# Mixed decoder layer on one core: heads of the scores in turn, a GpSimd drain, and other places for ten tiles' weight sums

## The chip, the cores and the metric

The kernel runs on one core of a Trainium2 chip. A core has five engines, each with its own instruction stream: TensorE (PE in the profile, with PEld for its weight loads), VectorE (DVE), ScalarE (ACT), GpSimd (POOL) and SyncE (SP), which issues most of the DMAs. The engines meet only at semaphores. The metric is the device time of one execution in microseconds (us); less is better.

## The reference

The program is one decoder layer on 512 tokens of 1024 features, all in float32. It has three parts, each with a normalisation before and after it and added to the input:

- a SwiGLU network ("first FFN"): `(silu(x @ w_gate) * (x @ w_up)) @ w_out`, with 2816 inner features, added by half;
- a token mixer: one projection `h @ w_in` to 3592 columns feeds four HGRN2 heads (a gated recurrence with a decay per feature) and four mLSTM heads (a gated recurrence with a stabilised exponential gate, query and key of 64 features, values of 128); both are causal. Their normalised, gated outputs go through `w_out`;
- a second FFN like the first.

For an mLSTM head the reference computes, chunk by chunk, with `D` made of the cumulated gates:

```
P = einsum("bhtd,bhsd->bhts", qc, kc) * exp(D - m_t)
num = inter * (qc @ C) + P @ vc
```

The product of `qc` and `kc` is what is called the scores here.

## The kernel before, in words

All products are made of float32 operands split into two parts of a rounded format ("high" and "low"), and three products high x high, high x low, low x high are added in PSUM. So every weight tile of 512 KB is loaded by SP into a raw buffer (line 242), cast by ScalarE (line 279, the high part) and subtracted by VectorE (line 281, the low part) into one of four prepared weight buffers, before TensorE uses it. `weights` plans the loads: each raw buffer belongs to a ring of three or five, and a load is issued when the buffer's last reader is done.

Both FFNs save products by Strassen-like sums, with seven products instead of eight. In the input products (`ffn_in`, `prod`, matmuls of line 602) the sums of weight tiles are made in SBUF by `tensor_tensor` additions of raw buffers (lines 291 to 295): VectorE makes most of them, GpSimd those of the first tiles. In the output products (`ffn_out`, `quartered`, lines 920 and 928) sums of quarters of weight tiles are needed, thirteen tiles for each FFN: eight for the first half of the output columns, five for the second. These are not made in SBUF. `sums_ahead` copies four quarters from the weights in DRAM into a DRAM buffer (`f1sums`, `f2sums`; three DMAs on SP, lines 868 to 870) and adds other quarters to it by three accumulating DMAs, each of which GpSimd issues (line 873) after the one before it has landed. A normal weight load brings the finished sums in later.

`sums_ahead` is a generator with four steps: copies, then one accumulate per step. `sums_due` names the tiles that are due, and each call of `make_sums` starts one more tile and takes one step of each tile in work. Before the change, the first FFN makes its thirteen tiles in its own products; the second FFN's first eight are made in the mixer (calls in the jobs for the convolution, `hi` and `mv`), and its last five in its own input products (every tenth product, `EVERY`) and at the start of its output products.

The order on each engine is the order in which the program's functions call the instructions; `behind` puts an instruction behind another one in that order (line 496). `self.loaded` is the last load issued so far.

The mixer runs a queue of "jobs", which are generators for the projection's products (`job_f`, `job_t`, matmuls of lines 185 to 187 and 532), and calls `fill(n)` to place `n` pieces of them between steps of the recurrences, so that TensorE has work. `mlstm_scores` goes through the four heads; the generator `mlstm_head` makes the exponential of a head's gates first (a matmul by `neg_m` at line 1489, VectorE, ScalarE, then GpSimd's `affine_select` at line 1515 as causal mask), then four 128x128 score products of 64 partitions at line 1523, and then the product of both on VectorE (line 1525). Heads 0 and 2 lie on partitions 0 to 63, heads 1 and 3 on 64 to 127. PSUM has eight banks, given out in turn by `ps`.

In `masks` GpSimd prepares constants for the mixer; the last instruction there is the copy at line 1236.

At the end of each half of the output products `rms` (lines 436 to 441) takes squares on ScalarE, whose sums GpSimd scales into small column tiles, for the normalisation.

Of the kernel before, what the change touches and what calls it, by code (L numbers as in the profile page):

```python
# [11 lines left out]
ALU = mybir.AluOpType  # L12
# [72 lines left out]
PLACES, LATER = {2: 1, 4: 2, 6: 0, 8: 3}, {7: (2, 3)}  # L85

AGAIN, ROWS = (10,), (18, 19, 20, 21)
EVERY = 5, 10

# [25 lines left out]
class Layer:  # L117
# [122 lines left out]

    def load(self, ld):
        self.loaded = self.nc.sync.dma_start(self.raw[ld.key], ld.src)

    def lie(self, kind):

# [10 lines left out]
    def split(self):  # L256

        nc = self.nc
        it = self.items.popleft()
        raw = self.raw[it.key]  # L260
        _, a, b = raw.shape
        if it.dst:
            w = it.dst()
        else:
            if self.wt is None:
                self.wt = self.wp.tile([P, 2 * D * WBUF + FRONT + PAD], F32R, name="w")
            if not self.slot and it.key[0] != "mix":
                self.free = deque(FREE2 if it.key[0] == "f2" else FREE)
            n, o = self.lie("out" if it.key[1] == "out" else "mix" if it.key[0] == "mix" and b == 512 else "any")
            self.free.remove(n)  # L270
            w = self.wt[:, o : o + 2 * D].rearrange("p (b k t) -> p b k t", b=2, k=a)
            self.slot[id(w)] = n, o, w
        hi, lo = self.both(w)
        if it.sums:
            raw, hi, lo = (self.flat(v)[:, QUARTER:] for v in (raw, hi, lo))
        self.ready.append((w, it.dst is not None))
        rows = it.rows
        if rows is None:
            nc.scalar.copy(hi, raw)  # L279
            yield  # L280
            self.low = nc.vector.tensor_tensor(lo, raw, hi.bitcast(F32), op=ALU.subtract)  # L281
        else:
            for j in range(a):
                nc.scalar.activation(hi[:, j], raw[:, j], AF.Copy, scale=rows[:, j : j + 1])
            yield
            for j in range(a):
                nc.vector.scalar_tensor_tensor(
                    lo[:, j], raw[:, j], rows[:, j : j + 1], hi[:, j].bitcast(F32), op0=ALU.mult, op1=ALU.subtract
                )
        with self.behind(*self.hold):  # L290
            for out, other in it.adds:
                o, c = self.raw[out], self.raw[other]

                late = out[1] >= (HEAD if out[0] == "f1" else 1)
                (nc.vector if late else nc.gpsimd).tensor_tensor(o, o, c, op=ALU.add)  # L295
        self.load_due(self.done)
        self.done += 1
        yield
# [482 lines left out]

    def ffn_in(self):

        self.sums_due("f2" if self.second else "f1", (1,) if self.second else (0, 1))
        for n, (p, t) in enumerate(ORDER2[len(HEADS2) :] if self.second else ORDER[len(HEADS) :]):
            if n > 14 and n % EVERY[self.second] == 0:
                self.make_sums()
            with self.behind(*(self.c22 if p == "p3" and self.second else ())):
                self.feed()
            self.c22 = []  # L790
            self.lag()
            self.prod(p, t)
            self.after(p, t)
            if t == PAIRS - 1 and p in ("p3", "p7"):
                self.hs.append(self.h_tile(len(self.hs)))
        self.feed()
        self.lag()
# [61 lines left out]
        parts = [t.rearrange("p k (c u t) -> p k u c t", u=2, t=P) for t in parts]  # L859
        return [[t[:, j // 2, j % 2] for j in range(4)] for t in parts]  # L860

    def sums_ahead(self, f, h, k2):

        nc, to = self.nc, self.sums_of[f, h, k2]
        w = (self.ffn1_w_out, self.ffn2_w_out)[f == "f2"][0]
        q = w[k2 * 2 * P : (k2 + 1) * 2 * P, h * 512 : (h + 1) * 512].rearrange("(k p) (c f) -> p k c f", p=P, f=QUARTER)
        with self.behind(self.loaded):
            nc.sync.dma_start(to[:, 0], q[:, 0, 1])
            nc.sync.dma_start(to[:, 1], q[:, 1, 0])
            nc.sync.dma_start(to[:, 2:], q[:, 1])  # L870
        yield
        for a, b, v in ((0, 2, q[:, 0, :1].broadcast_to([P, 2, QUARTER])), (2, 3, to[:, :1]), (3, 4, to[:, 2:3])):
            nc.gpsimd.dma_start(to[:, a:b], v, accum_op=ALU.add)  # L873
            yield

    def sums_due(self, f, halves):
        self.ahead, self.making = deque(k for k in self.sums_of if k[0] == f and k[1] in halves), []

    def make_sums(self):

        if self.ahead:
            self.making.append(self.sums_ahead(*self.ahead.popleft()))
        self.making = [g for g in self.making if next(g, self) is not self]

    def ffn_out(self, gpost_row, scale, after, trans, head):
# [81 lines left out]

        with self.behind(*([self.loaded] if self.second else [])):
            g = self.gain("gpost", gpost_row)
        n = 0  # L970
        for half in range(2):
            C = [[self.ps() for _ in range(2)] for _ in range(2)]
# [32 lines left out]
        for k2 in OUT[1][-LAST:]:  # L1005
            ws.append(self.pull())
            more(n + 1)
            n += 1
        hs = [made.popleft()[0] for _ in range(LAST)]

        add(C, T, 1)

# [33 lines left out]
    def job_f(self, name, then):  # L1046

        w, ps = self.pull(), self.ps()
        if name[0] == "c":
            self.make_sums()  # L1050
        for k in range(ND):
            self.in_k(ps, w, k, [(0, HALF), (HALF, T)])
            if k < ND - 1:
                yield
        self.drop(w)
        then(ps)
        self.got.add(name)
        yield
# [148 lines left out]
    def masks(self, mc, mb):  # L1207

        nc = self.nc

        self.mask = mb.tile([P, len(LEVELS), 64], I32, name="mask")
        nc.gpsimd.memset(self.mask, 1)
        for n, c in enumerate(LEVELS):
            m = self.mask[:, n, :].rearrange("p (b c) -> p b c", c=c)
            pat = [[-2 * c, 64 // c], [0, c]]
            nc.gpsimd.affine_select(m, m, pattern=pat, compare_op=ALU.is_ge, fill=0.0, base=0, channel_multiplier=1)
            pat = [[2 * c, 64 // c], [0, c]]
            nc.gpsimd.affine_select(m, m, pattern=pat, compare_op=ALU.is_ge, fill=0.0, base=c - 1, channel_multiplier=-1)
        self.eye = mb.tile([P, P], I32, name="eye")
        nc.gpsimd.memset(self.eye, 1)  # L1220
        nc.gpsimd.affine_select(
            self.eye, self.eye, pattern=[[1, P]], compare_op=ALU.is_equal, fill=0.0, base=0, channel_multiplier=-1
        )

        sel = mb.tile([4, 6, 2, 64], F32, tag="tmp", bufs=1, name="sel")
        nc.gpsimd.memset(sel, 1.0)
        self.sel = mc.tile([36, 6, P], F32R, name="selr")
        nc.gpsimd.memset(self.sel.bitcast(I32), 0)
        for n in range(6):
            pat = [[0, 2], [0, 64]] if n < 4 else [[-1, 2], [0, 64]]  # L1230
            base = -n if n < 4 else -2 * (n - 4)
            nc.gpsimd.affine_select(
                sel[:, n], sel[:, n], pattern=pat, compare_op=ALU.is_equal, fill=0.0, base=base, channel_multiplier=1
            )
        for r in (0, 32):
            nc.gpsimd.tensor_copy(self.sel[r : r + 4], sel.rearrange("p n a b -> p n (a b)"))
    def forget_gates(self, mb):

        nc = self.nc
# [187 lines left out]
    def job_rows(self):  # L1427

        ps = self.ps()[:100]
        for k in range(ND):  # L1430
            for n in range(2):
                for m in range(2):
                    v = slice(HALF * m, HALF * (m + 1))
                    self.nc.tensor.matmul(
                        ps[:, v], self.gw[:, k, :], self.xop(k, n, HALF * m, HALF * (m + 1)),
                        start=k + n + m == 0, stop=k == ND - 1 and n == 1, skip_group_check=True,
                    )
            if k % 2 == 1 and k < ND - 1:
                yield
# [64 lines left out]
    def mlstm_head(self, h):  # L1504
# [16 lines left out]
        for c in range(NT):  # L1521
            s = slice(c * P, (c + 1) * P)
            nc.tensor.matmul(sc[:, s], self.qk[o : o + 64, 2 + h // 2, s], self.qk[o : o + 64, h // 2, s], start=True, stop=True)  # L1523
        yield
        nc.vector.scalar_tensor_tensor(self.pT[:, h, :], sc, 0.125, e, op0=ALU.mult, op1=ALU.mult)
        yield

    def mlstm_scores(self, mc):
# [2 lines left out]
        self.nend = mc.tile([P, NH, NT], F32, name="nend")  # L1531
        self.pT = mc.tile([P, NH, T], F32, name="pT")
        H = [self.mlstm_head(h) for h in range(NH)]
        next(H[0])
        for h in range(NH):
            if h + 1 < NH:
                next(H[h + 1])
            self.fill(3)
            next(H[h])
            next(H[h])  # L1540
        w = mc.tile([P, NT, NH], F32, name="w")
        nc.vector.tensor_tensor(w, self.aT, self.nend.rearrange("p h c -> p c h"), op=ALU.add)
        nc.scalar.activation(w, w, AF.Exp)
# [127 lines left out]
    def mixer(self):  # L1671
        nc, tc = self.nc, self.tc
        self.got, self.jobs = set(), deque()
        self.sums_due("f2", (0,))
        with tc.tile_pool(name="ma", bufs=1) as ma:
            self.vh = ma.tile([P, NT, NH, P], F32, name="vh")
            self.vm = ma.tile([P, NT, NH, 129], F32, name="vm")
# [187 lines left out]
```

## Time and profile before

| what | value |
|---|---|
| three timed runs | 936.67, 940.88, 942.86 us (median 940.88) |
| the profiled execution | 936.0 us |
| its span, first to last instruction | 934.3 us |
| granted TensorE clock | 0.998 |
| DMA traffic | 142.28 MB, 152 GB/s in the mean |
| DMA issued by GpSimd (q0) | 13.64 MB, 11.2% of 16 engines |

The stages in the profiled execution: the first FFN's input products from the start to 224 us (first matmul of line 920), its output products and the norm behind them to 340 (first matmul of line 542), the mixer to about 600, the second FFN's input products to about 813, its output products to 927 (last matmul of line 920), and the last normalisation and stores.

The page has a line of busy time for each engine, the span in 40 slices, DMA queues, a chain of work followed back from the last instruction, and the costliest groups of instructions. Matmuls are pipelined and their ends are modelled, so TensorE's busy share alone does not say whether it runs at its pace; the number of matmuls in a stretch does. "idle before" is the time in which an engine did nothing ahead of an instruction, with what ended it.

### The profile page before, as it was taken

The numbers are of one execution on the slowest core, as the hardware profiler recorded it, in microseconds if no ns is written. First come the engines' busy times: TensorE is split into PE (matmuls) and PEld (weight loads), VectorE is DVE, ScalarE is ACT, GpSimd is POOL, SyncE is SP. The second block draws the span as 40 slices with busy tenths as digits, with TensorE's granted clock in tenths as the row PEclk, the third lists the DMA queues.
The fourth block names the chain that finished last, engine by engine and source line by source line (L and its number), as shares of the span: only waits on it lengthen the run. The fifth ranks groups of instructions, "written<-read, shape, count | busy, mean of one in ns | idle before, by whom it ended". The sixth has DMA issues, their size and how long they took to land.

```text
span 934.3 us, 18295 instructions
## 1 busy us (share of the span) xinstructions
PE 922.8 (99%) x7435; PEld 887.7 (95%) x7435; DVE 759.2 (81%) x980; ACT 521.5 (56%) x751; POOL 179.5 (19%) x250
## 2 busy tenths in 40 slices
PE   9999999999999999999999999999999999999996
PEld 7999999999999999998888887899999999999996
DVE  6899988889887786698766555799899889988883
ACT  7646455557566457956523345594445545756641
POOL 3531112211111045222230310313010010100001
PEclk9999999999999999999999999999999999999999
DMA  9255778766996234477742125253376556467522
GB/s 315 70 152 143 187 206 194 193 147 160 241 276 215 81 98 123 121 176 160 170 87 63 45 90 175 88 166 93 97 192 171 150 159 198 132 193 224 175 74 91
DMA packets 116494, 142.28 MB, mean 152 GB/s; under 512 B 7189, under 2 KB 89657, under 8 KB 116410
## 3 DMA queue, kind: packets, MB, share of 16 engines
q1 hardware_dynamic: 101562, 126.95, 43.8%
q0 software_dynamic: 14560, 13.64, 11.2%
q8 instruction: 58, 0.95, 0.4%
q10 hardware_dynamic: 288, 0.52, 0.2%
q14 instruction: 26, 0.21, 0.1%
HBM read 138.99 MB, written 29.36 MB: 180 GB/s over the span
## 4 chain that ended last, share of the span: by engine, by line
PE 54%; DVE 5%; issue 2%; DMA 2%; POOL 1%; ACT 1%; DVEq 0%; POOLq 0%; ACTq 0%
PE ps L602 14%; PE ps L928 7%; PE ps L532 6%; PE ps L920 5%; PE ps L185 5%; PE ps L187 5%; PE ps L186 5%; DVE w L281 2%; PE ps L1342 2%; DMA raw<-in_ffn_w_in_dram 2%; DVE raw L295 1%; PE ps L347 1%; POOL raw L295 1%; PE ps L542 1%; PE ps L1523 0%
## 5 line engine op out<-in xcount | busy, mean ns | idle before, releaser
L279 ACT CAST w<-raw 128x1024 fp32r<-128x1024 f32 x244 | 249.6, 1029 | 195.8 <-PE ps L602 85.5
L281 DVE TENSOR_TENSOR w<-raw,w 128x1024 fp32r<-128x1024 f32 x244 | 297.5, 1222 | 32.8 <-ACT w L279 31.5
L602 PE MATMUL ps<-xq,w 128*128 128x256 f32 x2016 | 237.3, 277 | 0.0
L602 PEld LDWEIGHTS ps<-xq,w 128*128 128x128 f32 x2016 | 232.9, 188 | 0.1
L602 PE MATMUL ps<-sq,w 128*128 128x256 f32 x1512 | 178.2, 276 | 2.2 <-DVE ps L621 1.8
L602 PEld LDWEIGHTS ps<-sq,w 128*128 128x128 f32 x1512 | 174.3, 188 | 3.2 <-issue 2.0
L295 DVE TENSOR_TENSOR raw<-raw,raw 128x1024 f32<-128x1024 f32 x72 | 89.8, 1251 | 11.8 <-DMA raw<-in_ffn_w_in_dram 10.3
L920 PE MATMUL ps<-w,hs 128*128 128x256 f32 x768 | 91.2, 276 | 0.0
L920 PEld LDWEIGHTS ps<-w,hs 128*128 128x128 f32 x768 | 88.9, 188 | 0.0
L185 PE MATMUL ps<-w,xq 128*128 128x512 f32 x192 | 78.0, 407 | 0.1
L928 PE MATMUL ps<-w,hs 128*128 128x256 f32 x624 | 75.0, 276 | 0.0
L186 PE MATMUL ps<-w,xq 128*128 128x512 f32 x192 | 74.9, 391 | 0.0
L187 PE MATMUL ps<-w,xq 128*128 128x512 f32 x192 | 74.8, 391 | 0.0
L928 PEld LDWEIGHTS ps<-w,hs 128*128 128x128 f32 x624 | 72.7, 188 | 0.0
L532 PE MATMUL ps<-xq,w 128*128 128x256 f32 x480 | 55.7, 277 | 0.0
L532 PEld LDWEIGHTS ps<-xq,w 128*128 128x128 f32 x480 | 54.9, 188 | 0.5 <-issue 0.5
L814 ACT CAST hs<-hf 128x1024 fp32r<-128x1024 f32 x34 | 35.8, 1053 | 34.2 <-PE ps L928 22.3
L815 DVE TENSOR_TENSOR hs<-hf,hs 128x1024 fp32r<-128x1024 f32 x34 | 41.5, 1221 | 11.9 <-ACT hs L814 11.5
L873 POOL DMA_DIRECT2D f1sums<-f1sums x26 | 22.8, 879 | 111.7 <-DMA f1sums<-in_ffn_w_out_dram 53.1
L185 PEld LDWEIGHTS ps<-w,xq 128*128 128x128 f32 x192 | 36.1, 188 | 8.5 <-issue 0.9
L187 PEld LDWEIGHTS ps<-w,xq 128*128 128x128 f32 x192 | 36.0, 188 | 8.1 <-DVE xq L354 0.3
L873 POOL DMA_DIRECT2D f2sums<-in_ffn_w_out_dram x13 | 17.3, 1333 | 137.3 <-DMA f2sums<-in_ffn_w_out_dram 137.3
(262 smaller groups left out, 1201.6 us busy)
## 6 DMA issues: line engine op xcount, KB each, us to landing
raw<-in_ffn_w_in_dram SPq DMA_DIRECT2D x98, 512.0 KB, 4.9
raw<-in_ffn_w_out_dram SPq DMA_DIRECT2D x44, 512.0 KB, 4.5
raw<-in_w_mix_in_dram SPq DMA_DIRECT2D x28, 512.0 KB, 4.1
raw<-f1sums SPq DMA_DIRECT2D x13, 512.0 KB, 7.5
raw<-f2sums SPq DMA_DIRECT2D x13, 512.0 KB, 4.5
raw<-in_w_mix_out_dram SPq DMA_DIRECT2D x8, 512.0 KB, 4.3
f1sums<-in_ffn_w_out_dram SPq DMA_DIRECT2D x26, 128.0 KB, 4.4
f1sums<-in_ffn_w_out_dram SPq DMA_DIRECT2D x13, 256.0 KB, 5.5
```

The source lines that it names most:

```text
L185: mm(ps, sh, mh, start=start, stop=False, **kw)
L186: mm(ps, sh, ml, start=False, stop=False, **kw)
L187: mm(ps, sl, mh, start=False, stop=stop, **kw)
L279: nc.scalar.copy(hi, raw)
L281: self.low = nc.vector.tensor_tensor(lo, raw, hi.bitcast(F32), op=ALU.subtract)
L295: (nc.vector if late else nc.gpsimd).tensor_tensor(o, o, c, op=ALU.add)
L532: mm(ps[:, u0:u1], w[:, a, k, :], self.xop(k, b, u0, u1), start=k + n + m == 0, stop=k == ND - 1 and n == 2, skip_group_check=True,)
L602: self.nc.tensor.matmul(ps[:, c], wb[b][:, k, v], left[d][:, k, :], start=first and a + n + k == 0, stop=n == 2 and k == KH - 1, skip_grou ...
L815: self.nc.vector.tensor_tensor(lo, src, hi.bitcast(F32), op=ALU.subtract)
L873: nc.gpsimd.dma_start(to[:, a:b], v, accum_op=ALU.add)
L920: mm(out, a[kk][:, i * P : (i + 1) * P], w[:, b, kk, QUARTER * v : QUARTER * (v + 1)], start=begin and c == kk == n == 0, stop=kk == 1 and ...
L928: mm(ps[:, QUARTER * c : QUARTER * (c + 1)], A[a][:, c], B[b], start=begin and c == n == 0, stop=n == 2, skip_group_check=True,)
```

## The change

The scores' products of two heads alternate, chunk by chunk, and the gates of the next two heads come ahead of them. Of the second FFN's thirteen tiles of sums, the copies for five are issued at the end of the first FFN, behind its last output weight load; their accumulates, and five more whole tiles, run in the mixer; all accumulates for the second FFN stand behind the masks. The last three tiles run in the second FFN's output products, and its input products make none. A drain instruction stands on GpSimd in the second FFN's input products, behind its weight additions.

```diff
-EVERY = 5, 10
+EVERY, EARLY, AHEAD = 5, 5, 10
...
     def load(self, ld):
         self.loaded = self.nc.sync.dma_start(self.raw[ld.key], ld.src)
+        if ld.key[:2] == ("f1", "out"):
+            self.loaded1 = self.loaded
...
                 late = out[1] >= (HEAD if out[0] == "f1" else 1)
-                (nc.vector if late else nc.gpsimd).tensor_tensor(o, o, c, op=ALU.add)
+                added = (nc.vector if late else nc.gpsimd).tensor_tensor(o, o, c, op=ALU.add)
+                if not late:
+                    self.added = added
...
     def ffn_in(self):
-        self.sums_due("f2" if self.second else "f1", (1,) if self.second else (0, 1))
+        nc = self.nc
+        if not self.second:
+            self.begun = ()
+            self.sums_due("f1")
         for n, (p, t) in enumerate(ORDER2[len(HEADS2) :] if self.second else ORDER[len(HEADS) :]):
-            if n > 14 and n % EVERY[self.second] == 0:
+            if n > 14 and n % EVERY == 0 and not self.second:
                 self.make_sums()
+            if n == 14 and self.second:
+
+                with self.behind(self.added):
+                    nc.gpsimd.drain()
...
-    def sums_ahead(self, f, h, k2):
+    def sums_ahead(self, f, h, k2, early=False):
         nc, to = self.nc, self.sums_of[f, h, k2]
-        w = (self.ffn1_w_out, self.ffn2_w_out)[f == "f2"][0]
+        w, last = (self.ffn1_w_out, self.ffn2_w_out)[f == "f2"][0], self.loaded1 if early else self.loaded
...
-        with self.behind(self.loaded):
+        with self.behind(last):
             nc.sync.dma_start(to[:, 0], q[:, 0, 1])
             nc.sync.dma_start(to[:, 1], q[:, 1, 0])
             nc.sync.dma_start(to[:, 2:], q[:, 1])
         yield
         for a, b, v in ((0, 2, q[:, 0, :1].broadcast_to([P, 2, QUARTER])), (2, 3, to[:, :1]), (3, 4, to[:, 2:3])):
-            nc.gpsimd.dma_start(to[:, a:b], v, accum_op=ALU.add)
+            with self.behind(*([self.selected] if f == "f2" else [])):
+                nc.gpsimd.dma_start(to[:, a:b], v, accum_op=ALU.add)
             yield
-    def sums_due(self, f, halves):
-        self.ahead, self.making = deque(k for k in self.sums_of if k[0] == f and k[1] in halves), []
+    def sums_due(self, f, n=None, done=0):
+        self.ahead, self.making = deque([k for k in self.sums_of if k[0] == f][done:n]), []
+
+    def copies_early(self):
+
+        self.begun = deque(self.sums_ahead(*k, early=True) for k in [k for k in self.sums_of if k[0] == "f2"][:EARLY])
+        for g in self.begun:
+            next(g)
     def make_sums(self):
-        if self.ahead:
+        if self.begun:
+            self.making += [self.begun.popleft() for _ in range(min(2, len(self.begun)))]
+        elif self.ahead:
             self.making.append(self.sums_ahead(*self.ahead.popleft()))
         self.making = [g for g in self.making if next(g, self) is not self]
...
     def ffn_out(self, gpost_row, scale, after, trans, head):
...
+        if self.second:
+            self.sums_due("f2", done=AHEAD)
...
         hs = [made.popleft()[0] for _ in range(LAST)]
+        if not self.second:
+            self.copies_early()
...
     def job_f(self, name, then):
-        if name[0] == "c":
+        if name in ("conv0", "conv1", "conv2", "conv3"):
             self.make_sums()
...
-            nc.gpsimd.tensor_copy(self.sel[r : r + 4], sel.rearrange("p n a b -> p n (a b)"))
+            self.selected = nc.gpsimd.tensor_copy(self.sel[r : r + 4], sel.rearrange("p n a b -> p n (a b)"))
...
     def job_rows(self):
         ps = self.ps()[:100]
+        self.make_sums()
...
     def mlstm_head(self, h):
...
             nc.tensor.matmul(sc[:, s], self.qk[o : o + 64, 2 + h // 2, s], self.qk[o : o + 64, h // 2, s], start=True, stop=True)
-        yield
+            yield
...
     def mlstm_scores(self, mc):
         H = [self.mlstm_head(h) for h in range(NH)]
         next(H[0])
-        for h in range(NH):
-            if h + 1 < NH:
+        next(H[1])
+        for h in range(0, NH, 2):
+            self.fill(3)
+            for g in H[h + 2 : h + 4]:
+                next(g)
+            self.fill(3)
+            for _ in range(NT + 1):
+                next(H[h])
                 next(H[h + 1])
-            self.fill(3)
-            next(H[h])
-            next(H[h])
...
     def mixer(self):
         self.got, self.jobs = set(), deque()
-        self.sums_due("f2", (0,))
+        self.sums_due("f2", AHEAD, EARLY)
```

## The prediction

> **What bounds the kernel now.** I read the page first, then busy time by stretches, then the waits.
>
> ```profile
> span 934.3 us, 18295 instructions
> ...
> PE 922.8 (99%) x7435; PEld 887.7 (95%) x7435; DVE 759.2 (81%) x980; ACT 521.5 (56%) x751; POOL 179.5 (19%) x250
> ```
>
> TensorE is the bound by its busy share, but ends of matmuls are modelled, so I check it by counts. Columns of the next view: stretch, its length, then busy time and (number of instructions) of PE, PEld, DVE, ACT, POOL, then clock, DMA share, GB/s.
>
> ```profile
> 60.00:300.00 240.00, 240.00 (x2117) 240.00 (x2116) 213.72 (x242) 135.70 (x178) 38.93 (x47) 1.00 0.76 199
> 304.00:340.00 36.00, 35.92 (x316) 35.72 (x316) 27.71 (x39) 18.49 (x41) 7.75 (x19) 1.00 0.17 50
> 380.00:405.00 25.00, 25.00 (x219) 24.52 (x218) 20.00 (x25) 19.70 (x24) 3.02 (x3) 1.00 0.52 130
> 660.00:750.00 90.00, 89.82 (x787) 89.31 (x786) 83.49 (x90) 45.27 (x55) 5.75 (x6) 1.00 0.52 141
> 750.00:780.00 30.00, 28.01 (x243) 27.45 (x242) 25.93 (x28) 13.05 (x16) 2.84 (x3) 1.00 0.64 179
> 780.00:815.00 35.00, 35.00 (x311) 35.00 (x310) 33.87 (x43) 24.05 (x34) 4.01 (x4) 1.00 0.56 153
> ```
>
> In the first FFN, 240 us hold 2117 matmuls: 0.1134 us each, without a hole. That is the pace to measure by. At it, 660 to 750 should hold 794 and holds 787 (0.8 us lost); 750 to 780 should hold 265 and holds 243 (2.4 us lost, 2.0 of them plainly idle). The granted clock is 1.00 throughout. So there is little to win: no matmul is removed, and only idle time of TensorE can go. The waits of PE name the one long one:
>
> ```profile
> PE ps L602 <- DVE ps L621: 1.8, 1, 1.8
> ```
>
> VectorE was late once, in the second FFN, where it is busy 25.93 + 33.87 of 65 us (92%) from 750 to 815. Why it was late is in the order of time there (start, length, engine, line; in brackets the idle time before it and what ended it):
>
> ```profile
> 749.31 0.51 SPq L868 DMA_DIRECT2D f2sums<-in_ffn_w_out_dram  x1
> ...
> 750.50 0.60 SPq L870 DMA_DIRECT2D f2sums<-in_ffn_w_out_dram  x1
> ...
> 752.49 20.68 SPq L242 DMA_DIRECT2D raw<-in_ffn_w_in_dram  x7
> ...
> 754.47 1.17 POOL L873 DMA_DIRECT2D f2sums<-in_ffn_w_out_dram  x1 [22.61 <-DMA f2sums<-in_ffn_w_out_dram]
> ...
> 759.96 1.23 DVE L295 TENSOR_TENSOR raw<-raw,raw 128x1024 f32<-128x1024 f32 x1 [3.50 <-DMA raw<-in_ffn_w_in_dram]
> ```
>
> Three copies for one tile's sums stand on SP from 749.31 to 751.10, the weight loads behind them go on at 752.49, an accumulating DMA joins at 754.47, and VectorE's add then waits 3.50 us for a weight load. The 1.8 us wait of TensorE follows some ten microseconds later.
>
> **The change, part by part.** The base is the profiled execution: 936.0 us, of which the span is 934.3. The median of the three runs, 940.88, is 4.9 above it.
>
> *Sums out of the second FFN's input products.* Four sets of three copies and twelve accumulating DMAs leave the stretch from 683 to 800; SP's weight loads then follow each other there unbroken. The hole above goes: **-2.0 us**. It is bounded by 0 (the load would have been late anyway: only one of the four sets led to a hole) and by -3.2 (2.4 + 0.8, all that both stretches lost).
>
> *Scores of two heads in turn.* The products of 64 partitions (heads 0 and 2 in the lower half, 1 and 3 in the upper) now alternate between the halves.
>
> ```profile
> L1523 PE MATMUL ps<-qk 64*128 64x128 f32 x32 | 4.6, 285 | 0.0
> ...
> L1388 PE MATMUL ps<-q,kk 128*128 128x128 f32 x32 | 3.9, 275 | 0.0
> ```
>
> ```profile
> L1523 PE MATMUL ps<-qk x32: 272/272/373, 486.5 to 497.7; 64*128 64x128 f32 x32
> ```
>
> ```profile
> 490.10 0.74 PEld L1523 LDWEIGHTS ps<-qk 64*128 64x128 f32 x6 [0.35 <-issue]
> ```
>
> Head by head, 32 of them take 4.6 us, no less than 32 of full height (3.9). No row shows halves in turn. If a pair ran beside each other, half would go: -2.3. If each change of half cost what the longest of a group has over the shortest (373 - 272 ns), the 28 changes more would add 2.8. The nearest rows, those of L1523 itself, say neither gain nor loss; since each pair shares no partition and no bank, I take some overlap, **-1.0**. The visits to such small products between the projection's matmuls fall from six to five; one begins with 0.35 us of idle weight loading: **-0.2** (0 to -0.35). Queued behind the later scores are VectorE's four multiplies into pT; they share the order with one weight split, which four prepared weight buffers cover.
>
> The Trainium skill, TensorEngine Tiling (Array Packing), Key Properties, says that tiles of the array on different rows can load weights and multiply in parallel, and that a change of the tiling mode drains the array. By it this term would be about -2.3 (an estimate), 1.3 below what I take; no run here shows it yet.
>
> *Five tiles copied early.* Fifteen DMAs go to SP behind the first FFN's last weight load:
>
> ```profile
> 303.88 2.26 SPq L242 DMA_DIRECT2D raw<-in_ffn_w_out_dram  x1
> 340.96 0.37 SPq L242 DMA_DIRECT2D raw<-in_w_mix_in_dram  x1
> ```
>
> ```profile
> raw<-in_w_mix_in_dram SPq DMA_DIRECT2D x28, 512.0 KB, 4.1
> ...
> f2sums<-in_ffn_w_out_dram SPq DMA_DIRECT2D x13, 256.0 KB, 5.7
> f2sums<-in_ffn_w_out_dram POOLq DMA_DIRECT2D x13, 256.0 KB, 6.1
> f2sums<-f2sums POOLq DMA_DIRECT2D x26, 128.0 KB, 4.1
> ```
>
> SP is idle from 306.1 to 340.96, and the DMA share from 304 to 340 is 0.17. At 0.6 us an issue they need 9 us; even five sets landing one after another (5 x 5.7) end 6 us before the next load. **0**; were they later than that, the first mixer loads would be late by the excess.
>
> *Thirty accumulates in the mixers, not 24.* They stay behind the masks on POOL, where they stood before:
>
> ```profile
> 377.65 3.29 POOL L1236 CAST selr<-sel 4x768 fp32r<-4x768 f32 x2
> 394.95 1.24 POOL L873 DMA_DIRECT2D f2sums<-in_ffn_w_out_dram  x1 [14.02 <-DMA f2sums<-in_ffn_w_out_dram]
> ...
> 484.44 0.94 POOL L873 DMA_DIRECT2D f2sums<-f2sums  x1 [2.59 <-ACT vm L1696]
> 485.42 1.40 POOL L1548 MEMSET C<- 128x1548 f32 x1
> 486.77 0.83 POOL L1515 TENSOR_SCALAR_AFFINE_SELECT e<-e 128x512 f32<-128x512 f32 x1
> ```
>
> POOL sat 14.02 us until copies came; now five tiles lie ready at 381, and their accumulates need not wait for each other. Behind them POOL has C's memset and the selects for the scores; they have been kept until 485, and six more accumulates of 1 us with a 14 us earlier start end no later. The new thing is the burst at 381: four or five accumulates at once beside weight loads. A weight gives 48 matmuls, 5.4 us; with three raw buffers a load has 16 us, of which it needs 4.1. Even doubled it stays hidden: **0**, at most +2 where one load would take over 16.
>
> *Three tiles in the output products.* The trace has this case: the first FFN issues its last three sets in the same turns.
>
> ```profile
> 226.54 0.50 SPq L868 DMA_DIRECT2D f1sums<-in_ffn_w_out_dram  x1
> ...
> 251.65 0.65 SPq L868 DMA_DIRECT2D f1sums<-in_ffn_w_out_dram  x1
> ```
>
> ```profile
> 232.95 1.17 POOL L873 DMA_DIRECT2D f1sums<-in_ffn_w_out_dram  x1 [7.18 <-DMA f1sums<-in_ffn_w_out_dram]
> ...
> 280.60 0.81 POOL L873 DMA_DIRECT2D f1sums<-f1sums  x1 [5.91 <-DMA f1sums<-f1sums]
> 281.17 0.48 POOL L437 TENSOR_SCALAR col<-col 128x1 f32<-128x1 f32 x1
> ```
>
> ```profile
> 240.00:281.00 41.00, 41.00 (x364) 41.00 (x363) 35.81 (x42) 25.25 (x31) 6.95 (x8) 1.00 0.95 271
> ```
>
> Nine accumulates take 47.7 us, and TensorE has 364 matmuls in 41 us, its full pace, at a DMA share of 0.95. So **0**. The next rival says what it costs when this cover is gone.
>
> *The drain.* One POOL instruction, with no semaphore, behind the four adds; POOL then idles anyway:
>
> ```profile
> 689.16 1.25 POOL L873 DMA_DIRECT2D f2sums<-in_ffn_w_out_dram  x1 [45.06 <-DMA f2sums<-in_ffn_w_out_dram]
> ```
>
> It fits into 45 us: **0**.
>
> Sum: 936.0 - 2.0 - 1.0 - 0.2 = **932.8** on the profile's scale. What puts the other runs up to 6.9 above it (942.86 - 936.0) the trace cannot show. If it is late weight loads like the one above, the median comes down to 932.8; if it is something else, it stays 4.9 higher, 937.7. I take the middle, **935**.
>
> **The rivals.**
>
> *Everything pays.* Pairs overlap fully (-2.3, -0.35), both FFN stretches fill up (-3.2), and the runs' spread goes with them: 936.0 - 5.9 = 930.1. For it: the cause at 749 is plain. Against it: small waits of TensorE on VectorE stay.
>
> *Nothing but the scores.* VectorE at 92% is late by itself, and the hole moves to the next late load: 936.0 - 1.2 = 934.8 as profiled, 939.7 as a median. For it: VectorE also waited for loads around 653, with no copies near.
>
> *POOL's chain ends too late (slower).* Place: the end of the output products' first half, where POOL's small sums stand behind the ninth accumulate, and ScalarE's squares behind those (twelve column buffers, two to a square: six squares run free).
>
> ```profile
> 870.20 0.19 POOL L437 TENSOR_SCALAR col<-col 128x1 f32<-128x1 f32 x1 [46.08 <-ACT junk L436]
> ```
>
> ```profile
> 815.40 0.42 SPq L158 DMA_DIRECT2D gpost<-in_norm_post_dram  x1
> ```
>
> The last row is that of the first FFN's sums, all their DMAs together, from issue to landing:
>
> ```profile
> DMA to landing us min/median/max: 3.1/5.7/9.6
> ```
>
> The first set follows the load at 815.40 and lands by 822; at 5.3 us a step (47.7 / 9) the chain ends at 870, as POOL is first asked. Up to 7 us a step (885) prepared weights, three or four at 5 us, cover it. At the longest landing, 9.6 plus 1 for the issue, it ends at 917: 917 - 885 = 32 us lost, 936.0 - 3.2 + 32 = 965. From 7.4 us a step on (889, 4 lost against 3.2 won) the change is slower than before. Against it: the first FFN, at a fuller DMA, did it in 5.3.
>
> The Trainium skill, DMA: Bandwidth & Descriptors, Queues, rings and completion order, has each DMA engine alternate between its queues by packets, so that accumulates and loads slow each other. The trace agrees in part: all DMAs of the first FFN's sums land at a median of 5.7 us, at 9.6 at the longest.
>
> **How the numbers follow.** Forecast, 931.5 to 938: 0.50. Everything pays, 929 to 931.5: 0.28. Nothing but the scores, 938 to 943: 0.12. POOL's chain, 943 to 965: 0.10. The range 929 to 943 leaves out the last and the edge of the second. One per cent, about what a measurement of this kernel can tell from no change, is 9.4 us: 931.5 and 950.3. So faster 0.28, same 0.62, slower 0.10.
>
> **What would show it.** Right: 265 matmuls in each 30 us from 680 to 800 and no wait of PE on L621 over 1 us; scores' 32 products under 4 us busy; POOL's first accumulate at 381; SP copies at 304 to 316 with no hole of TensorE at 340. Wrong: POOL's first column sum after 875; a wait of TensorE between 381 and 420; weight loads of the second FFN still landing late without any copies near.

## The result, and the profile after

The changed kernel takes 932.64 us (median of six runs, 932.12 to 934.34), the kernel before 938.96 beside it. The ratio is 0.9931, 95% interval 0.9908 to 0.9954: 6.3 us faster, less than one per cent. In two later comparisons on other chips it was 0.9947 (0.9929 to 0.9965) and 0.9944 (0.9923 to 0.9965), a gain of 4.5 and 5.1 us, so about 5 us is the better figure. The profiled execution took 932.28, 3.7 less than that of before.

The head of the page, changed kernel:

```profile
span 930.6 us, 18289 instructions
...
PE 921.0 (99%) x7435; PEld 886.6 (95%) x7435; DVE 759.3 (82%) x980; ACT 521.7 (56%) x751; POOL 178.4 (19%) x250
```

The same matmuls are there, so the gain has to be idle time. Busy time by stretches, changed kernel (columns as in the prediction):

```profile
304.00:340.00 36.00, 36.00 (x318) 35.85 (x316) 27.67 (x39) 18.57 (x40) 7.74 (x19) 1.00 0.46 128
380.00:405.00 25.00, 25.00 (x217) 24.52 (x217) 20.00 (x25) 19.78 (x23) 15.10 (x16) 1.00 1.02 182
660.00:750.00 90.00, 89.91 (x791) 89.69 (x790) 84.42 (x90) 46.59 (x56) 0.00 (x0) 1.00 0.40 123
750.00:780.00 30.00, 28.99 (x251) 28.43 (x250) 26.60 (x28) 13.31 (x16) 0.00 (x0) 1.00 0.46 142
780.00:815.00 35.00, 35.00 (x311) 35.00 (x310) 33.91 (x44) 23.57 (x33) 0.00 (x0) 1.00 0.39 113
815.00:870.00 55.00, 55.00 (x488) 55.00 (x487) 47.39 (x61) 33.59 (x47) 9.28 (x12) 1.00 0.90 254
```

GpSimd has left the second FFN's input products from 660 on, but 750 to 780 holds 251 matmuls, not the 265 of full pace; before, 243. By idle time about half of the hole is still there (1.01 us of 1.99), by matmuls 14 of 22. The wait of TensorE on VectorE is 0.8 us instead of 1.8, because VectorE still waits 2.82 us for a weight load (3.50 before), though no copy is near (waits of PE, then the order of time):

```profile
PE ps L606 <- DVE ps L625: 0.8, 1, 0.8
```

```profile
757.51 1.23 DVE L297 TENSOR_TENSOR raw<-raw,raw 128x1024 f32<-128x1024 f32 x1 [2.82 <-DMA raw<-in_ffn_w_in_dram]
```

To find all of the 3.7 us I set pieces of the chain that ended last beside each other, pieces that both kernels have. First the kernel before, then the changed one (start, length, piece):

```profile
353.17 32.64 PE ps L532 x288
...
600.31 2.82 PE ps L602 x24
...
826.90 38.08 PE ps L928 x336
...
899.66 27.21 PE ps L920 x240
```

```profile
353.57 32.64 PE ps L536 x288
...
599.31 2.82 PE ps L606 x24
...
824.46 38.08 PE ps L948 x336
...
897.22 27.21 PE ps L940 x240
```

The differences, after minus before:

| from | to | difference in the stretch |
|---|---|---|
| start | the mixer's first products, 353 | +0.40 |
| there | the second FFN, 600 | -1.40 |
| there | its output products, 827 | -1.44 |
| there | its last 240 products, 900 | 0.00 |
| there | the end of the span | -1.26 |

The second row holds the scores, the third the input products that the sums have left. The +0.40 of the first is there long before the first edit has an effect: the 501st matmul starts at 65.07 in the kernel before and at 65.47 in the changed one, and in all traces here at 64.82 to 66.36. The last row is a surprise: nothing that the prediction priced lies behind 900.

### The profile page after: what moved, and what is told of

Its sections match the earlier page's. It is cut to its first block, busy times and chain, and to the rows that moved or that the text cites. A ratio compares the mean times of both kernels' runs of the same rounds, so it can differ in the third digit from the quotient of the medians.

```text
span 930.6 us, 18289 instructions
## 1 busy us (share of the span) xinstructions
PE 921.0 (99%) x7435; PEld 886.6 (95%) x7435; DVE 759.3 (82%) x980; ACT 521.7 (56%) x751; POOL 178.4 (19%) x250
## 4 chain that ended last, share of the span: by engine, by line
PE 58%; DVE 2%; DMA 2%; issue 1%; ACT 1%; POOL 0%; DVEq 0%; POOLq 0%; ACTq 0%; SPq 0%
PE ps L606 19%; PE ps L948 7%; PE ps L536 6%; PE ps L940 5%; PE ps L185 5%; PE ps L186 4%; PE ps L187 4%; PE ps L1366 2%; DMA raw<-in_ffn_w_in_dram 2%; DVE w L283 1%; PE ps L351 1%; PE ps L546 1%; PE ps L1459 0%; PE ps L1664 0%; PE ps L1637 0%
## 5 line engine op out<-in xcount | busy, mean ns | idle before, releaser
L885 POOL DMA_DIRECT2D f2sums<-in_ffn_w_out_dram x13 | 16.7, 1398 | 195.1 <-DMA f2sums<-in_ffn_w_out_dram 195.1
```

## The experiments

All kernels below compute the whole reference. The kernels of a group shared a chip and the runs of the kernel before.

### Each part alone, and the pairing taken apart

Scores alone: the kernel before with only this edit.

```diff
-        yield
+            yield
...
-        for h in range(NH):
-            if h + 1 < NH:
...
+        for h in range(0, NH, 2):
...
+            for _ in range(NT + 1):
+                next(H[h])
                 next(H[h + 1])
...
```

> The kernel before with the scores of two heads in turn alone. Theory (the pairs overlap, and the placement of the sums is a gain of its own): 2.0 us under the kernel before in the median, near 937, with its spread of several us between runs kept; the 32 score products are busy 2.3 us instead of 4.6. Rival (the spread of the kernel before comes from the scores): near 932.6 with a spread of about 2 us.

The other parts alone: the changed kernel with those lines put back.

> The changed kernel with the scores head by head again. Theory: 2.0 us over the changed kernel, near 934.6, with its small spread of about 2 us; the 32 score products busy 4.6 us. Rival (the sums' new places are worth nothing by themselves): near 937 to 939, spread over 5 us.

Pairs from one half:

```diff
-        H = [self.mlstm_head(h) for h in range(NH)]
+        H = [self.mlstm_head(h) for h in (0, 2, 1, 3)]
```

> The changed kernel with its pairs drawn from the same half of the array: heads 0 and 2 in turn, then 1 and 3. Five visits as in the changed kernel, but nothing that could run beside each other. Theory (the two halves work beside each other): the 32 products are busy 4.6 us again, and the time is 2 us over the changed kernel, near 934.6. Rival (fewer visits and longer groups give the gain): 2.3 us busy and near 932.6.

No drain:

```diff
-            if n == 14 and self.second:
-                with self.behind(self.added):
-                    nc.gpsimd.drain()
```

> The changed kernel without the drain on GpSimd. Theory: no difference, 932.6 within 0.7. Rival (the drain keeps something of GpSimd apart in the second FFN): over 934.

| kernel | median us | ratio to before (937.55) |
|---|---|---|
| scores alone | 934.97 (933.31 to 938.89) | 0.9976 (0.9958 to 0.9993) |
| the rest alone | 935.02 (933.06 to 936.89) | 0.9970 (0.9956 to 0.9984) |
| pairs from one half | 935.06 (933.06 to 937.13) | 0.9972 (0.9959 to 0.9986) |
| no drain | 934.17 (932.99 to 935.96) | 0.9962 (0.9950 to 0.9975) |

The 32 score products, groups by line and form; one fence each for the changed kernel, the rest alone, and pairs from one half:

```profile
L1548 PE MATMUL ps<-qk 64*128 64x128 f32 x32 | 2.3, 285 | 0.0
```

```profile
L1548 PE MATMUL ps<-qk 64*128 64x128 f32 x32 | 4.6, 285 | 0.0
```

```profile
L1548 PE MATMUL ps<-qk 64*128 64x128 f32 x32 | 4.1, 278 | 0.0
```

Two heads in turn within one half save 0.5 of 4.6 us; from different halves, 1.8 more. One product takes as long as ever (285 ns), so it is the pair that runs at once. The starts in the traces say the same without the modelled ends: within one half the products start 112 ns apart, as they do head by head, and the 0.5 us comes from two long groups instead of four short ones; between halves the second of a pair starts 7 ns behind the first, and the pairs are 112 ns apart. From the mixer's first products to the second FFN, the six traces with pairs from two halves take 245.5 to 245.7 us, pairs from one half 246.9, and three head by head (the kernel before, the rest alone, and "accumulates put off" below) 247.1 to 247.3. Scores alone and the rest alone (the drain is in it) are worth 2.6 and 2.5 us, and their sum, 5.1, is about the whole. The spread of the kernel before stayed with the scores alone (5.6 us) and was smaller with the rest alone (3.8). The time without the drain decided nothing here: 934.17 is 1.5 over the changed kernel's first 932.64, but that was on another chip.

### Copies and accumulates, each in its place

The changed kernel once more, and beside it: ten tiles begun in the mixer (`EARLY` 0 instead of 5); copies left in the second FFN with their accumulates put off; copies early with their accumulates left there.

> The changed kernel once more, on one chip with the three kernels beside it, since without its drain it stood 3.4 us under the kernel before on one chip, and itself 6.3 us under it on another. Theory (the drain is worth nothing, the chip and the few runs made the difference): 3 to 4 us under the kernel before. Rival (the drain is worth something): 5 to 6.5 us under it.

> The changed kernel with all ten tiles begun in the mixer, none copied behind the last weight load of the first FFN; thirteen turns for ten tiles. Theory (SP and the DMA engines have room in the mixer): the same as the changed kernel within 0.7 us, and GpSimd's first accumulate near 395 instead of 381. Rival (the copies in the mixer delay its weight loads as those in the second FFN did): 1.5 to 2.5 us over the changed kernel, with idle time of TensorE between 380 and 480.

```diff
-EVERY, EARLY, AHEAD = 5, 5, 10
+EVERY, EARLY, AHEAD = 5, 0, 10
```

> The kernel before with the twelve copies of four tiles left in the second FFN's input products and their accumulates put off to the output products. Theory (the copies on SP's queue push the weight loads back): no gain, near the kernel before, and VectorE's add near 760 still waits over 3 us for its load. Rival (the accumulates, which share the DMA engines with the loads, make them late): 1.4 us or more under the kernel before, as far as the second FFN goes.

```diff
             if n > 14 and n % EVERY[self.second] == 0:
-                self.make_sums()
+                if self.second:
+                    if self.ahead:
+                        self.making.append(self.sums_ahead(*self.ahead.popleft()))
+                        next(self.making[-1])
+                else:
+                    self.make_sums()
```

> The kernel before with the copies of the second half's five tiles moved behind the last weight load of the first FFN, and their accumulates left in the second FFN's input products. Theory (the copies are what hurts there): 1.4 us or more under the kernel before. Rival (the accumulates): near the kernel before.

```diff
-            self.making.append(self.sums_ahead(*self.ahead.popleft()))
+            k = self.ahead.popleft()
+            self.making.append(self.a_turn_later(self.begun[k]) if k[:2] == ("f2", 1) else self.sums_ahead(*k))
...
+        if not self.second:
+            self.copies_early()
```

| kernel | median us | ratio to before (937.58) |
|---|---|---|
| changed | 933.07 (931.65 to 934.55) | 0.9947 (0.9929 to 0.9965) |
| ten begun in the mixer | 941.03 (939.01 to 948.99) | 1.0045 (1.0023 to 1.0067) |
| accumulates put off | 937.32 (935.97 to 940.46) | 0.9997 (0.9982 to 1.0011) |
| copies early, accumulates left | 956.80 (956.28 to 958.42) | 1.0204 (1.0184 to 1.0224) |

**Ten begun in the mixer** cost 8 us, against my theory. GpSimd in order of time, then TensorE:

```profile
395.46 1.24 POOL L885 DMA_DIRECT2D f2sums<-in_ffn_w_out_dram  x1 [14.45 <-DMA f2sums<-in_ffn_w_out_dram]
...
498.48 0.81 POOL L885 DMA_DIRECT2D f2sums<-f2sums  x1 [2.54 <-DMA f2sums<-f2sums]
499.33 1.39 POOL L1577 MEMSET C<- 128x1548 f32 x1
500.67 2.41 POOL L1540 TENSOR_SCALAR_AFFINE_SELECT e<-e 128x512 f32<-128x512 f32 x4
```

```profile
502.11 0.79 PE L1514 MATMUL ps<-nm,selr 36*128 36x512 f32 x1 [6.06 <-DVE pT L1550]
```

The first accumulate comes at 395 as expected, behind its copy. Then the thirty steps go nearly one by one, each when the step before it has landed, 10 us for a tile, though the last copy was issued by 456; the chain ends at 499.29. All four selects for the scores stand behind it, VectorE's multiply waits for them, and TensorE idles 6.06 us. The weight loads, which the rival named, had no part in it: up to there TensorE has lost nothing. The clock (0.88 in this stretch) adds to the loss:

```profile
480.00:504.00 24.00, 17.94 (x95) 13.21 (x94) 9.30 (x24) 6.98 (x11) 8.29 (x10) 0.88 0.42 66
```

From 498.19 on the trace grants half the clock for 10.24 us, so the wait costs more than its own length. In the changed kernel the chain starts 14 us earlier, with five tiles ready at once whose steps go between each other, 22.5 us for all five; it ends 28 us earlier, with 7 us to spare before the memset:

```profile
381.29 4.32 POOL L885 DMA_DIRECT2D f2sums<-in_ffn_w_out_dram  x4
...
470.84 0.81 POOL L885 DMA_DIRECT2D f2sums<-f2sums  x1 [2.61 <-DMA f2sums<-f2sums]
478.74 1.39 POOL L1577 MEMSET C<- 128x1548 f32 x1 [7.08 <-DVE sT L1371]
```

**Accumulates put off** is no test: they were not put off. They are called later, but the DMA view from 683 to 800 shows as many of them as in the kernel before:

```profile
f2sums<-in_ffn_w_out_dram POOLq DMA_DIRECT2D x4, 256.0 KB, 6.0
f2sums<-f2sums POOLq DMA_DIRECT2D x8, 128.0 KB, 3.4
```

So the order on an engine is not simply the order of the calls, as the kernel's description has it. On GpSimd it seems to go by when an instruction is ready, which the next run bears out.

**Copies early, accumulates left** went the same way, further: with their copies ready, the accumulates moved up to 316, ahead of the small column sums of the first FFN's end.

```profile
344.64 0.81 POOL L875 DMA_DIRECT2D f2sums<-f2sums  x1 [2.17 <-DMA f2sums<-f2sums]
345.22 0.91 POOL L439 TENSOR_SCALAR col<-col,col 128x1 f32<-128x1 f32 x2
```

```profile
300.00:340.00 40.00, 33.14 (x293) 32.95 (x291) 19.59 (x22) 11.68 (x16) 11.82 (x12) 0.96 0.92 184
340.00:380.00 40.00, 26.46 (x210) 25.66 (x211) 22.69 (x34) 17.55 (x41) 18.39 (x32) 0.82 0.40 95
```

20.4 us of TensorE's 80 are idle there. All sums are done by 510, so this trace has none of them in the second FFN either, and its time from there to the output products, 224.3 us, is the shortest of all. And it shows what the line `behind(self.selected)` in the change is for: the early copies may be made only if the accumulates are held back by an instruction of their own engine.

### The queue or the traffic, and the drain again

Copies of the second half's tiles from ScalarE's queue, within 10 us of their old times; copies early and accumulates held behind GpSimd's four adds of the second FFN; and the changed kernel beside its twin without the drain.

```diff
-        with self.behind(self.loaded):
-            nc.sync.dma_start(to[:, 0], q[:, 0, 1])
...
+        act = (f, h) == ("f2", 1)
+        eng = nc.scalar if act else nc.sync
+        with self.behind(self.high if act else self.loaded):
+            eng.dma_start(to[:, 0], q[:, 0, 1])
...
```

> The kernel before with the copies for the second half's five tiles issued by ScalarE instead of SyncE, each set behind a cast of ScalarE at about the same time; accumulates unchanged. Theory (the copies hurt by standing in SP's queue ahead of weight loads): as in the changed kernel's second FFN, 2 to 2.5 us under the kernel before, and no late load beside the sets at 690 to 815. Rival (it is their traffic, from whichever queue): equal to the kernel before, the waits of VectorE for weight loads as long as there.

```diff
-            nc.gpsimd.dma_start(to[:, a:b], v, accum_op=ALU.add)
+            with self.behind(*([self.added] if early else [])):
+                nc.gpsimd.dma_start(to[:, a:b], v, accum_op=ALU.add)
```

> The kernel before with the copies for the second half's five tiles behind the first FFN's last weight load, and the fifteen accumulates left in the second FFN's input products, now in one run behind GpSimd's four adds there (near 655). Theory (copies hurt, accumulates do not): 2 to 2.5 us under the kernel before. Rival (any traffic of the sums there makes loads late): no better than the kernel before, the lost matmuls between 655 and 720 where the accumulates now are.

> The changed kernel on one chip with its twin that lacks the drain. Theory: 933 to 934.5, equal to the twin within 0.7 us. Rival (the drain is worth about 1 us): 1 us or more under the twin.

> The changed kernel without the drain, beside the changed kernel itself. Theory: equal to it within 0.7 us. Rival: 1 us or more over it.

| kernel | median us | ratio to before (938.26) |
|---|---|---|
| copies from ScalarE | 938.80 (936.57 to 941.76) | 1.0007 (0.9992 to 1.0023) |
| accumulates behind the adds | 949.38 (946.23 to 951.43) | 1.0110 (1.0085 to 1.0134) |
| changed | 933.17 (931.67 to 934.80) | 0.9944 (0.9923 to 0.9965) |
| no drain | 933.55 (932.46 to 936.04) | 0.9949 (0.9930 to 0.9968) |

**Copies from ScalarE**: no gain, and the hole stays, larger; VectorE waits 4.05 us for its load there, 3.50 before (by stretches, then TensorE):

```profile
750.00:780.00 30.00, 27.29 (x219) 26.63 (x219) 24.10 (x26) 11.58 (x15) 2.84 (x3) 0.94 0.63 173
```

```profile
773.93 1.34 PE L602 MATMUL ps<-sq,w 128*128 128x256 f32 x5 [2.54 <-DVE ps L621]
```

So it is not that SP's loads stand behind SP's copies alone; of the two theories, the one left is the traffic of the sums, from whichever queue. Of the 24 matmuls fewer than in the kernel before, idle time (0.72 us more) makes about six; most of the rest is the clock, one half for 3.41 us from 774.00 on, 0.94 in the mean of the stretch. (This kernel also loses 1.7 us between 353 and 405, away from the edit, and the cause is open; so only the hole is read here.)

**Accumulates behind the adds** stand dense. GpSimd in order of time, DMA issues from 650 to 666, then VectorE and TensorE:

```profile
646.63 4.73 POOL L878 DMA_DIRECT2D f2sums<-in_ffn_w_out_dram  x4
```

```profile
raw<-in_ffn_w_in_dram SPq DMA_DIRECT2D x5, 512.0 KB, 16.7
```

```profile
673.33 1.23 DVE L297 TENSOR_TENSOR raw<-raw,raw 128x1024 f32<-128x1024 f32 x1 [14.67 <-DMA raw<-in_ffn_w_in_dram]
```

```profile
676.34 1.86 PE L606 MATMUL ps<-xq,w 128*128 128x256 f32 x7 [6.82 <-DVE w L283]
```

A weight load beside them takes a median of 16.7 us from issue to landing. In the changed kernel it is 4.8 in the same stretch (three loads), and from 683 to 800, without sums, 4.2:

```profile
raw<-in_ffn_w_in_dram SPq DMA_DIRECT2D x24, 512.0 KB, 4.2
```

The wait is again not the whole loss, as the clock of 0.83 says:

```profile
660.00:690.00 30.00, 22.26 (x164) 21.56 (x162) 16.67 (x18) 9.01 (x11) 5.72 (x8) 0.83 0.62 142
```

My theory that accumulates do no harm there fell; four issued at once are denser than anything that the kernel before had there. How the kernel before divides its harm between the two kinds stays open; no run took out one kind alone at the old density.

**The drain.** The two medians differ by 0.4 us in runs that spread over 3, which decides nothing. The traces do. From the start of the last 240 products (the chain) to the end of the span; no drain, then the rest alone:

```profile
span 931.3 us, 18288 instructions
...
896.61 27.21 PE ps L936 x240
```

```profile
span 933.9 us, 18289 instructions
...
900.51 27.21 PE ps L940 x240
```

That is 34.69 without it and 33.39 with it. The changed kernel has 33.38, the kernel before 34.64. From the last matmul's start to the end, the six traces with the drain take 6.41 to 6.43 us, the eight without it 7.68 to 7.73. The records that a page does not count as busy tell why (start and length in us):

```
before     GpSimd DRAIN  927.98  5.51     SyncE's last DRAIN  932.21     GpSimd goes on  933.53
no drain   GpSimd DRAIN  924.94  5.54     SyncE's last DRAIN  929.17     GpSimd goes on  930.52
changed    GpSimd DRAIN  640.65  6.66     (beside an add that ends at 643.08)
           GpSimd DRAIN  925.54  1.42     SyncE's last DRAIN  929.77     GpSimd goes on  929.81
```

Every program here ends with a drain of each engine, and all wait for the last. Without the early drain, GpSimd's takes 5.5 us and ends 1.3 us after SyncE's, which waited for the outputs to land. With it, the end drain takes 1.42 us and is done before they have landed. So my theory fell: the early drain moves 4 us of draining under other work, and 1.3 us of it had been exposed.

## Why the prediction was right or wrong

The forecast of 935 lies 2 us above the three medians of the changed kernel (932.64, 933.07, 933.17), and its sum on the profile's scale, 932.8, half a microsecond above the 932.28 measured. The sum is closer than its terms, and that is luck: against its 3.2 us the sums gave 0.56 less and the scores 0.20 more in this pair of traces, the start lost 0.40 by scatter, and the drain, which was not priced, brought 1.26.

- **Sums out of the input products, -2.0: the size about right, the mechanism half right.** The step said that the hole goes; 0.82 of its 1.80 us stay, since the load behind it is late without any sums near, which the prediction had named as a sign of being wrong. That was the rival "nothing but the scores", true by half; what makes that load late is open. This pair of traces gives -1.44 from 600 to 827. But the nine traces without sums there take 224.3 to 227.2 us (mean 225.7), the four with them at the old density 226.6 to 228.6 (mean 227.5): 1.9 less, 1.5 if "copies from ScalarE" is left out, and the ranges overlap.
- **Scores, -1.0, and fewer visits, -0.2: near, -1.40.** The products themselves reached the outer bound, 2.3 us saved of 4.6. By the rule that I weighed (the Trainium skill, TensorEngine Tiling (Array Packing), Key Properties: tiles on different rows work in parallel), the trace agrees. "The nearest rows say neither gain nor loss" was the weak step: rows of one half cannot show what two halves do. From 353 to 600, 1.40 remains of it here, 1.6 in the mean of the traces above; where the rest of the 2.3 goes was not traced.
- **Early copies, 0, and thirty accumulates, 0: right together, not apart.** SP's fifteen issues end at 318, 23 us before the next load (below), and GpSimd's burst at 381 raised the DMA share to 1.02 without a wait of TensorE. But the second zero rests on the first, as the step said with its "14 us earlier start"; what it cost if that cover were gone it did not say: 8 us, not through the loads but through the selects.

```profile
317.41 0.60 SPq L881 DMA_DIRECT2D f2sums<-in_ffn_w_out_dram  x1
341.36 0.37 SPq L242 DMA_DIRECT2D raw<-in_w_mix_in_dram  x1
```

- **Three tiles in the output products, 0: right.** Nine accumulates take 820.34 to 867.61, 5.25 us a step against 5.3 in the first FFN, and TensorE has 488 matmuls in 55 us, as many as before. The first column sum follows without a pause; the slower rival did not occur, and had some 17 us to go by its own sum (885):

```profile
820.34 1.25 POOL L885 DMA_DIRECT2D f2sums<-in_ffn_w_out_dram  x1 [177.25 <-DMA f2sums<-in_ffn_w_out_dram]
...
866.80 0.81 POOL L885 DMA_DIRECT2D f2sums<-f2sums  x1 [5.85 <-DMA f2sums<-f2sums]
867.75 0.19 POOL L441 TENSOR_SCALAR col<-col 128x1 f32<-128x1 f32 x1
```

- **The drain, 0: the step that failed, -1.26.** It does fit into idle time, as said. What it changes elsewhere, at the program's end, was not asked.
- **From the profile to the median, the middle between 932.8 and 937.7: the lower end was right.** The spread shrank: 935.37 to 942.93 in 84 runs of the kernel before, 931.65 to 934.80 in eighteen of the changed one. That it came from late weight loads fits, but no trace of a slower run of the kernel before shows it. Their clocks hint at it, no more: in its 78 later runs the 33 with a mean granted clock of 0.997 or less take 939.15 in the median, the 45 others 937.10, as if a hole had now and then grown long enough to cost clock; the changed kernel's runs all have 0.998 or 0.999. The late loads did not vanish, as another execution of the changed kernel shows, where the load near 655 came 3.72 us late (2.36 in the first) and TensorE lost 1.20 us:

```profile
659.53 1.22 DVE L297 TENSOR_TENSOR raw<-raw,raw 128x1024 f32<-128x1024 f32 x1 [3.72 <-DMA raw<-in_ffn_w_in_dram]
```

```profile
676.96 1.30 PE L606 MATMUL ps<-sq,w 128*128 128x256 f32 x9 [1.20 <-DVE ps L625]
```

No kernel here beats the changed one.

## What to carry to other kernels

Transfers that nobody waits for belong where the loads beside them have slack: the same accumulates cost nothing at a DMA share of 0.9 to 1.0 in the mixer and the output products, and 1.5 to 2 us, or far more when issued densely, in a stretch at half that share whose loads land just in time. A hole of the matmul engine is to be priced with what it does to the clock: 1.80 us cost itself, 2.54 us cost half the clock for 3.4 us more. When a step is priced at nothing because of what hides it, price the same step without that cover, and look past its own place, to the end of the program too. Where the order on an engine is not that of the calls, a line moved in the code may stay where it was, or go far ahead, unless an instruction of that engine holds it, and only the trace tells whether an experiment did what its text says.

## What the runs showed of the hardware

- Two row halves of TensorE work beside each other on float32 products of 64 x 128 x 128: 32 of them take 2.32 us in turn between halves, 4.10 in turn within one half, 4.62 head by head.
- Four traces have a wait of TensorE over 2.1 us, of 2.54 (copies from ScalarE), 6.06 (ten begun in the mixer), 6.82 (accumulates behind the adds) and 18.04 us (copies early, accumulates left). In the wait or at its end begins a stretch in which half the clock is granted, of 3.41, 10.24, 10.24 and 17.07 us. The ten others, with no wait over 1.80 us, have the whole clock from 13 us to 927, and a further wait of 2.02 us in the last of the four was followed by none.
- GpSimd's drain at the end of the program took 5.5 us, and 1.42 when another, of 6.66 us, had run 285 us earlier. What it drains (its many DMAs, or its instructions in general) was not tried.
- Weight loads of 512 KB landed in 16.7 us (median of five) beside a run of accumulating DMAs, the first four of them issued at once; without them in 4.8 us in the same stretch (three) and 4.2 later (24). The Trainium skill, DMA: Bandwidth & Descriptors, Queues, rings and completion order, has each DMA engine alternate between its queues by packets; that a change of queue did not help agrees with it.
